# A one-core hybrid decoder trunk: the stores of activation pairs and their sums, in the up projection, go out on GpSimd's queue instead of SyncE's

## The chip, the cores and the metric

The kernel runs on one core of a Trainium2 chip. The metric is the device time of one execution, in microseconds (us). SyncE (SP) computes nothing here: it issues the kernel's DMA transfers, each after a wait for its semaphores, strictly in the order in which they stand on its queue. GpSimd (POOL), VectorE (DVE), ScalarE (ACT) and TensorE (PE) each run their own list of instructions, also in order.

## The reference, cut to what matters

One layer over 2048 tokens of width 1024: a mixer (sliding-window attention beside a gated recurrence), then a gated MLP of inner width 2816 with a causal convolution of three taps. Only the MLP matters here:

```python
h = rms_norm(x, ffn_norm_g[l]) * (1 + scale_f) + shift_f
u, v = jnp.split(h @ w_up[l], 2, axis=-1)          # 1024 -> 2 x 2816
u = causal_depthwise_conv(u, conv_w[l], conv_b[l])
x = x + gate_f * ((jax.nn.silu(u) * v) @ w_down[l])
```

## The kernel before, in words

All matmuls are made in float32 from a high and a low part of each operand: ScalarE rounds the high part (names ending in `h`), VectorE subtracts it for the low one (`l`), and three matmuls are added (`mm3`). Large products are split in 2 x 2 blocks and made with seven block products instead of eight, so that sums and differences of blocks have to be formed beforehand; GpSimd forms those of the weights.

**Up projection.** Two halves of 1024 tokens (`hf_`), and in each 22 blocks of 128 columns (`ff`) of both halves of w_up. For a column block, `prep_up` loads two raw weight tiles on SP (`wu_0r` and `wu_1r`, 512 KB each), GpSimd makes `s<-wu_1r`, `wu_1r<-wu_0r,wu_1r`, `s<-s,wu_0r` and, after VectorE has split them, a last `s<-wu_0r,s`. The splits are `wus`, `wvs`, `ws` and `w`. TensorE then runs seven products of 12 matmuls each into `ps_u`, in the order 1, 7, 2, 6, 5, 4, 3; product 1 uses `wus`, product 7 `wvs`. `up` adds the products, applies the convolution and the gate, and leaves the block's activations in `cc`.

**The pair of activations.** After every second block, `combine_a` forms on GpSimd the sums that the down projection's block products want: four operations, `sm<-cc,cc`, `cc<-cc`, `sm<-sm,cc`, `sm<-cc,sm`. Three stores follow, to a tensor in HBM, `act_d`, one for each pair: the second block `b` (512 KB), the first block `a`, which the second operation has changed (512 KB), and the three sums `sm` (768 KB). The first store needs nothing of GpSimd, the second its second operation, the third its fourth.

**What else is on these queues.** In half 1 `combine_w` makes the down projection's weight sums, one block for each `ff` up to 17 and two for each of 18 and 19: a load `cw` on SP, four operations `ct` on GpSimd, a store `wc_d` on SP. In half 0 `combine_t` does the like for the second half's inputs, four times. The raw tiles of `wu`, `cw` and `ct` share four buffers.

**Down projection.** It reads `act_d` (loads `da`) and the weights and their sums (loads `Sr` and `dw`, three to a block of weights), splits them (`S_0h`, `S_0l` and so on; `Th`, `Tl`) and multiplies into `ps_d`. Its first unit of work needs weights of all eleven blocks and the activations of half 0 only.

The order of instructions on each engine is made by a scheduler, which in the up projection is free to move what is independent; the numbers on a name (`act_d1_2`) are half and pair, on `cw0_7` output half and block.

Of the kernel before, what the change touches and what calls it, by code (L numbers as in the profile page):

```python
# [53 lines left out]
def kernel(ctx, tc, x, c, ada_w, ada_b, mix_norm_g, w_in, b_in, attn_sinks, attn_out_g,  # L54
# [3 lines left out]
    V, S, G, TE, SY = (InOrder(tc, e) for e in (nc.vector, nc.scalar, nc.gpsimd, nc.tensor, nc.sync))  # L58
# [21 lines left out]
    act_d = [[dram.tile([P, HT // 256, 7, P], F32, name=f"act_d{i}_{j}") for j in range(NJ)] for i in range(T // HT)]  # L80
# [1095 lines left out]
    def combine_acts(hf_, ff):  # L1176
        if len(acts) == 2:
            combine_a(hf_, ff // 2, *acts)
            acts.clear()

    def combine_a(hf_, j, c0, c1):


        a, b = (c.rearrange("p (t s n) -> p t s n", s=2, n=P) for c in (c0, c1))
        sm = gp_.tile([P, HT // 256, 3, P], F32, tag="gate", name=f"sm{hf_}_{j}")
        G.tensor_tensor(out=sm[:, :, 0, :], in0=a[:, :, 1, :], in1=b[:, :, 1, :], op=ALU.add)
        G.tensor_tensor(out=a[:, :, 1, :], in0=a[:, :, 0, :], in1=a[:, :, 1, :], op=ALU.subtract)
        G.tensor_tensor(out=sm[:, :, 1, :], in0=sm[:, :, 0, :], in1=a[:, :, 0, :], op=ALU.subtract)
        G.tensor_tensor(out=sm[:, :, 2, :], in0=b[:, :, 0, :], in1=sm[:, :, 1, :], op=ALU.subtract)
        for i, t in ((2, b), (0, a), (4, sm)):  # L1190
            SY.dma_start(out=act_d[hf_][j][:, :, i:i + (3 if i == 4 else 2), :], in_=t)

    def combine_t(k):

# [331 lines left out]
```

## Time and profile before

| | us |
|---|---|
| median of three runs | 2515.71 |
| lowest and highest of them | 2512.38, 2517.46 |
| the profiled execution's own time | 2515.02 |
| its span, from first to last instruction | 2513.2 |
| up projection, approximately | 1160 to 1992 of the span |
| down projection, approximately | 1997 to the end |

The mean granted clock of TensorE over the span was 0.970 of full speed. The profiled execution lies 0.69 us below the median and 1.8 us above its own span, so positions in the trace can be set directly against the times. Every store of `act_d` was issued by SP; GpSimd issued no transfer at all.

### The profile page before, as it was taken

To read this page: it belongs to the slowest core of one execution; us is meant where nothing else is said; L and a number is where in the kernel's file an instruction comes from. 1 tells how busy PE (TensorE), PEld (TensorE's weight loads), DVE (VectorE), ACT (ScalarE), POOL (GpSimd) and SP (SyncE) were. 2 spreads that over 40 slices of the span, in tenths; PEclk is the share of its full clock that TensorE was granted. 3 is DMA by queue.
4 is the path that set the end of the run, shared out by engine and by line. 5 is a ranking of instruction groups with operands and counts; after the bars stand their busy time and mean duration, and the time that the engine had idled before them with its cause. 6 is when DMAs were issued, how large, how long until landed. Compare 5 with 4: busy or idle time off the path is not lost.

```text
span 2513.2 us, 35666 instructions
## 1 busy us (share of the span) xinstructions
PE 2330.0 (93%) x13369; PEld 2013.4 (80%) x13369; DVE 1875.4 (75%) x2743; ACT 1057.2 (42%) x1776; POOL 880.9 (35%) x677
## 2 busy tenths in 40 slices
PE   5889898998989899999999998999999789998997
PEld 4778787887878788888888886778888579997997
DVE  8888778788876876578777778577776676677665
ACT  3336434623733454554333334233333254455443
POOL 6222212222312221215765653677777410011000
PEclk8999999999999999999999999999999889998999
DMA  7243233323322256654434436455545487787776
GB/s 211 89 118 97 80 90 95 94 67 101 97 65 82 86 179 222 230 190 125 138 122 142 122 109 201 138 156 159 159 147 159 136 306 231 214 279 261 261 245 201
DMA packets 361592, 389.90 MB, mean 155 GB/s; under 512 B 14069, under 2 KB 292555, under 8 KB 361419
## 3 DMA queue, kind: packets, MB, share of 16 engines
q1 hardware_dynamic: 361419, 387.62, 49.0%
q8 instruction: 105, 1.72, 0.3%
q14 instruction: 68, 0.56, 0.1%
HBM read 293.71 MB, written 93.86 MB: 154 GB/s over the span
## 4 chain that ended last, share of the span: by engine, by line
PE 60%; DVE 13%; DMA 10%; POOL 8%; issue 5%; ACT 3%; SPq 1%; DVEq 0%; ACTq 0%; POOLq 0%
PE ps_u L46 16%; PE ps_d L46 15%; PE ps_o L46 6%; PE lv L46 3%; PE ps_hg L46 3%; PE ps_hf L46 3%; PE ps_hq L46 3%; PE ps_i L46 2%; PE att_o L46 2%; POOL s L46 2%; DVE ada L46 2%; DMA Sr<-wc_d 1%; PE ps_q L46 1%; POOL wu_1r L46 1%; DVE AT L46 1%
## 5 line engine op out<-in xcount | busy, mean ns | idle before, releaser
L46 DVE TENSOR_TENSOR Tl<-da,Th 128x896 fp32r<-128x896 f32 x176 | 198.1, 1133 | 121.3 <-ACT Th L46 120.4
L46 ACT ACTIVATE Th<-da 128x896 fp32r<-128x896 f32 x176 | 166.3, 949 | 197.2 <-PE ps_d L46 158.8
L46 DVE SCALAR_TENSOR_TENSOR cc<-ub,cols,cc 128x1024 f32<-128x1024 f32 x88 | 150.1, 1706 | 19.6 <-ACT cc L46 17.4
L46 PE MATMUL lv<-a_q,K 128*128 128x128 f32 (+2 forms) x768 | 80.0, 264 | 44.4 <-DVE K L46 40.7
L46 PEld LDWEIGHTS lv<-a_q,K 128*128 128x128 f32 (+2 forms) x768 | 71.9, 176 | 56.9 <-DVE K L46 29.0
L46 POOL TENSOR_TENSOR s<-wu_0r,s 128x512 f32<-128x512 f32 x44 | 68.2, 1550 | 116.5 <-DVE ws_0l L46 14.8
L46 POOL TENSOR_TENSOR s<-wu_1r 128x512 f32<-128x512 f32 x44 | 69.7, 1584 | 87.8 <-DMA wu_1r<-in_w_up_dram 17.6
L46 ACT ACTIVATE cc<-cc 128x1024 f32<-128x1024 f32 x44 | 46.7, 1061 | 113.7 <-DVE cc L46 113.7
L46 DVE TENSOR_TENSOR cc<-cc,v 128x1024 f32<-128x1024 f32 x44 | 59.7, 1357 | 44.8 <-ACT cc L46 44.8
L46 POOL MEMSET AT<- 128x512 f32 x16 | 8.5, 533 | 232.1 <-PE ho L46 210.1
L46 POOL TENSOR_TENSOR wu_1r<-wu_0r,wu_1r 128x512 f32<-128x512 f32 x44 | 85.2, 1936 | 3.1
L46 POOL TENSOR_TENSOR pl<-raw,ph 128x512 fp32r<-128x512 f32 x32 | 45.4, 1419 | 101.2 <-ACT ph L46 85.6
L46 POOL TENSOR_SCALAR rv_d<-ssd 128x2 f32<-128x2 f32 x8 | 1.5, 193 | 209.3 <-DVE ssd L46 209.3
L46 POOL TENSOR_TENSOR s<-s,wu_0r 128x512 f32<-128x512 f32 x44 | 74.6, 1696 | 0.0
L46 DVE TENSOR_TENSOR v<-ps_u,v 128x512 f32<-128x512 f32 x88 | 60.4, 687 | 19.0 <-PE ps_u L46 15.7
L46 POOL TENSOR_TENSOR S_0l<-Sr,S_0h 128x512 fp32r<-128x512 f32 x1 | 2.6, 2600 | 202.2 <-ACT S_0h L46 202.2
L46 DVE COPY_PREDICATED AT<-lev,lv 128x512 f32<-128x512 uint32 (+1 forms) x96 | 69.8, 727 | 2.4 <-PE lv L46 1.2
L46 ACT ACTIVATE cc<-ub,cols 128x1024 f32<-128x1024 f32 x44 | 54.6, 1240 | 31.8 <-DVE ub L46 31.8
L46 DVE TENSOR_TENSOR ada<-ada,cond 128x1024 f32<-128x1024 f32 (+1 forms) x37 | 55.1, 1489 | 14.5 <-DMA ada<-in_ada_w_dram 13.1
L46 DVE TENSOR_TENSOR a_q<-a_q,tot 128x256 f32<-128x256 f32 x96 | 52.2, 544 | 11.8 <-PE lv L46 10.6
L46 DVE TENSOR_TENSOR ub<-ps_u,u 128x512 f32<-128x512 f32 x88 | 60.0, 682 | 0.1
L46 DVE TENSOR_TENSOR ot<-ps_o,gate 128x512 f32<-128x512 f32 x32 | 22.0, 688 | 47.7 <-PE ps_o L46 47.2
(2136 smaller groups left out, 9113.4 us busy)
## 6 DMA issues: line engine op xcount, KB each, us to landing
da<-act_d SPq DMA_DIRECT2D x176, 448.0 KB, 4.6
wu_0r<-in_w_up_dram SPq DMA_DIRECT2D x44, 512.0 KB, 3.7
wu_1r<-in_w_up_dram SPq DMA_DIRECT2D x44, 512.0 KB, 4.1
act_d<-cc SPq DMA_DIRECT2D x44, 512.0 KB, 5.9
ada<-in_ada_w_dram SPq DMA_DIRECT2D x40, 512.0 KB, 6.3
act_d<-sm SPq DMA_DIRECT2D x22, 768.0 KB, 4.7
x<-in_x_dram SPq DMA_DIRECT2D x26, 512.0 KB, 5.6
Sr<-wc_d SPq DMA_DIRECT2D x18, 512.0 KB, 7.1
```

Of the source, the lines that this page charges most:

```text
L46: ins = fn(*args, **kwargs)
```

## The change

One word: the three stores of `combine_a` are issued by `G` (GpSimd) instead of `SY` (SP). There are 66 of them, two `cc` and one `sm` for each of 22 pairs.

```diff
         for i, t in ((2, b), (0, a), (4, sm)):
-            SY.dma_start(out=act_d[hf_][j][:, :, i:i + (3 if i == 4 else 2), :], in_=t)
+            G.dma_start(out=act_d[hf_][j][:, :, i:i + (3 if i == 4 else 2), :], in_=t)
```

What the scheduler makes of it is seen in the order of instructions, here in three places. First SP's queue, in half 1, around the third pair (`act_d1_2`), before and after in one piece; the same piece recurs for every pair of half 1 up to the eighth.

```order
 L46 DMA wu1_8_0r_14678<-in_w_up_dram 128x8x128
 L46 DMA wu1_8_1r_14680<-in_w_up_dram 128x8x128
-L46 DMA act_d1_2_102<-cc1_5_14514 512x1x256
-L46 DMA act_d1_2_102<-cc1_4_14372 512x1x256
-L46 DMA act_d1_2_102<-sm1_2_14553 512x1x384
 L46 DMA cw0_7r_14812<-in_w_down_dram 128x2x512
 L46 DMA wc_d0_7_118<-ct0_7r_14814 128x1024
```

The load `cw0_7r`, which stood behind the three stores, now stands directly behind the weight load.

Second, GpSimd's list at the same pair.

```order
 L46 TENSOR_TENSOR s1_7_14536<-s1_7_14536,wu1_7_0r_14528 128x512
 L46 TENSOR_TENSOR sm1_2_14553<-cc1_4_14372,cc1_5_14514 128x4x128
+L46 DMA act_d1_2_102<-cc1_5_14514 512x1x256
 L46 TENSOR_TENSOR cc1_4_14372<-cc1_4_14372 128x4x128
 L46 TENSOR_TENSOR sm1_2_14553<-sm1_2_14553,cc1_4_14372 128x4x128
+L46 DMA act_d1_2_102<-cc1_4_14372 512x1x256
 L46 TENSOR_TENSOR sm1_2_14553<-cc1_5_14514,sm1_2_14553 128x4x128
+L46 DMA act_d1_2_102<-sm1_2_14553 512x1x384
 L46 TENSOR_TENSOR s1_7_14536<-wu1_7_0r_14528,s1_7_14536 128x512
 L46 TENSOR_TENSOR ct0_7r_14814<-cw0_7r_14812 128x256 x2
```

The three stores now stand among and behind the four sums, and ahead of the weight operations `s` and `ct` that come next. At the last pair of half 0 the operation `s1_1<-wu1_1_1r` stands ahead of the third store, elsewhere all three stand as here.

Third, SP's queue at the step from the up to the down projection.

```order
 L46 DMA da0_0_0_16944<-act_d0_0_89 128x896
-L46 DMA act_d1_10_110<-cc1_21_16833 512x1x256
-L46 DMA act_d1_10_110<-cc1_20_16724 512x1x256
-L46 DMA act_d1_10_110<-sm1_10_16839 512x1x384
 L46 DMA Sr0_1_16950<-in_w_down_dram 128x256
 L46 DMA Sr0_1_16950<-in_w_down_dram 128x512
```

The loads of the down projection's second block of weights (`Sr0_1`) and all behind them stood behind the stores of the last pair, and now stand behind none.

## Rows read from the trace of the kernel before

**Rows 1.** The page, part 1: busy us (share of the span) x instructions, one engine

```profile
PE 2330.0 (93%) x13369; PEld 2013.4 (80%) x13369; DVE 1875.4 (75%) x2743; ACT 1057.2 (42%) x1776; POOL 880.9 (35%) x677
```

**Rows 2.** Windows: us, busy of PE, PEld, DVE, ACT, POOL; clock, DMA share, GB/s

```profile
1380.00:1480.00 100.00, 100.00 (x439) 82.03 (x438) 78.69 (x84) 34.91 (x37) 61.91 (x37) 1.00 0.42 126
...
1680.00:1780.00 100.00, 99.35 (x434) 80.95 (x433) 74.57 (x78) 33.58 (x37) 79.29 (x53) 1.00 0.49 154
...
1980.00:2080.00 100.00, 75.00 (x471) 68.95 (x470) 68.58 (x64) 46.52 (x50) 16.64 (x10) 0.83 0.74 257
```

**Rows 3.** Waits of SP's queue, 1090 to 1985: total us, times, longest

```profile
SPq L46 <- DVE cc L46: 67.0, 8, 11.9
SPq L46 <- POOL cc L46: 62.7, 16, 5.4
...
SPq L46 <- POOL sm L46: 47.9, 25, 3.0
```

**Rows 4.** Timeline of SP's queue: start us, us, engine, line, operation, out<-in

```profile
1699.23 0.57 SPq L46 DMA_DIRECT2D cw_7r<-in_w_down_dram  x1
...
1988.03 0.36 SPq L46 DMA_DIRECT2D da<-act_d  x1
1996.65 4.94 SPq L46 DMA_DIRECT2D act_d<-cc  x2
2004.50 0.51 SPq L46 DMA_DIRECT2D act_d<-sm  x1
2005.07 1.67 SPq L46 DMA_DIRECT2D Sr<-in_w_down_dram  x2
```

**Rows 5.** Timeline of GpSimd; in brackets idle time before and what ended it

```profile
1567.90 2.02 POOL L46 TENSOR_TENSOR s<-wu_1r 128x512 f32<-128x512 f32 x1 [6.75 <-DMA wu_1r<-in_w_up_dram]
...
1616.43 2.28 POOL L46 TENSOR_TENSOR sm<-sm,cc 128x512 f32<-128x512 f32 x1
...
1627.14 1.43 POOL L46 TENSOR_TENSOR ct_3r<-cw_3r 128x256 f32<-128x256 f32 x2 [4.81 <-DMA cw_3r<-in_w_down_dram]
...
1695.05 1.30 POOL L46 TENSOR_TENSOR sm<-sm,cc 128x512 f32<-128x512 f32 x1
...
1704.64 1.92 POOL L46 TENSOR_TENSOR ct_7r<-cw_7r 128x256 f32<-128x256 f32 x2 [3.81 <-DMA cw_7r<-in_w_down_dram]
...
1709.02 1.29 POOL L46 TENSOR_TENSOR s<-wu_1r 128x512 f32<-128x512 f32 x1
...
1748.04 1.30 POOL L46 TENSOR_TENSOR s<-wu_1r 128x512 f32<-128x512 f32 x1
...
1943.89 2.51 POOL L46 TENSOR_TENSOR ct_9r<-cw_9r 128x256 f32<-128x256 f32 x2 [6.79 <-DMA cw_9r<-in_w_down_dram]
...
2003.20 1.28 POOL L46 TENSOR_TENSOR sm<-cc,sm 128x512 f32<-128x512 f32 x1
```

**Rows 6.** Timeline of TensorE in half 1

```profile
1572.40 0.80 PE L46 MATMUL ps_u<-t_T3h,wvs_1h 128*128 128x512 f32 x1 [7.53 <-ACT wvs_1h L46]
...
1675.07 0.51 PE L46 MATMUL ps_u<-t_T3h,wvs_6l 128*128 128x512 f32 x1 [0.32 <-DVE wvs_6l L46]
...
1909.18 0.50 PE L46 MATMUL ps_u<-t_T3h,wvs_18l 128*128 128x512 f32 x1 [0.30 <-DVE wvs_18l L46]
```

**Rows 7.** Timeline of ScalarE at the step to the down projection

```profile
2011.46 1.70 ACT L46 ACTIVATE S_1h<-Sr 128x1792 fp32r<-128x1792 f32 x1 [13.67 <-DMA Sr<-wc_d]
```

**Rows 8.** Timeline of VectorE at the same step

```profile
2013.19 2.02 DVE L46 TENSOR_TENSOR S_1l<-Sr,S_1h 128x1792 fp32r<-128x1792 f32 x1 [11.21 <-ACT S_1h L46]
```

**Rows 9.** One window of 10 us, columns as in Rows 2

```profile
2010.00:2020.00 10.00, 5.95 (x27) 5.81 (x28) 6.05 (x4) 6.38 (x5) 0.00 (x0) 0.51 1.03 400
```

**Rows 10.** Operations that touch act_d: duration ns min/median/max, first and last start

```profile
L46 SPq DMA_DIRECT2D act_d<-cc x44: 513/525/1247, 1163.2 to 2001.1; - x44
```

**Rows 11.** Timelines of VectorE and TensorE in half 0, at block 18

```profile
1453.05 1.22 DVE L46 TENSOR_TENSOR wvs_18l<-wu_1r,wvs_18h 128x1024 fp32r<-128x1024 f32 x1
...
1463.38 0.39 PE L46 MATMUL ps_u<-t_T3h,wvs_18l 128*128 128x512 f32 x1
```

## The prediction

> **What bounds the kernel now.** TensorE is busy 93% of the span [rows 1], but that share is an average, so I read the windows next. In half 0 it is busy 100 us of 100 at the full clock [rows 2]: nothing but fewer matmuls could shorten that stretch, and the change can only harm it. In half 1 it is busy 99.35 of 100, and GpSimd, at 79.29, is the fullest I see it. At the step to the down projection TensorE is busy 75 of 100, with the clock down to 0.83. So whatever can be gained lies in half 1 and at the two seams.
>
> Then the waits of SP's queue. Between 1090 and 1985 SP stood 67.0 us for `cc` of VectorE, 62.7 us for `cc` of GpSimd and 47.9 us for `sm` of GpSimd [rows 3]. Those are the operands of the moved stores. SP is otherwise idle enough, so the waits themselves cost nothing; they cost where a load that somebody wants stands behind them. The timelines show four kinds of such places:
>
> - *the step to the down projection.* SP issued the first block's loads by 1988.4, then stood for the last pair: stores at 1996.65 and 2004.50, the next weight load at 2005.07 [rows 4]. GpSimd's last sum began at 2003.20 and took 1.28 us [rows 5]: it is what released SP. ScalarE meanwhile stood 13.67 us for `Sr` [rows 7], VectorE 11.21 us for ScalarE's `S_1h` [rows 8].
> - *the seam of the halves.* GpSimd stood 6.75 us for `wu_1r`, which was issued behind the last pair of half 0; TensorE stood 7.53 us in the sequel [rows 5, 6].
> - *one early and one late pair of half 1*, where GpSimd stood 4.81 us for `cw_3r` and 6.79 us for `cw_9r` [rows 5].
> - *the steady pairs of half 1.* GpSimd stood 3.81 us for `cw_7r`, which SP issued at 1699.23, right behind the sums' store [rows 4, 5]. From one pair to the next the same operation on GpSimd comes at 1709.02 and 1748.04, so its loop takes 39.02 us; TensorE waits only 0.32 us once in a loop, for the low half that follows from GpSimd's work [rows 5, 6]; between the first of these waits and the last, both shown, lie five more, so there are seven such pairs. GpSimd thus sets the pace here, by a hair.
>
> **The change part by part.** It takes 66 issues off SP, some 0.53 us each [rows 10], 35 us in all; SP had idle time everywhere, so this by itself is worth nothing. It puts 66 issues on GpSimd, 3 for each pair. Call one issue's time on GpSimd *d*. No row shows d, since GpSimd issued nothing before. SP's shortest, 0.51 us [rows 10], is my lower bound. Of the rows on GpSimd itself, its sum over the same tile takes 1.30 us when it is undisturbed and 2.28 us when it is not, the same operation one pair apart [rows 5]. I take d = 1.3 us, because its undisturbed operation is the commonest row of GpSimd's own pace and lies between the ends, keep 2.28 us as the upper bound, and write 3d for a pair: 3.9 us at the value taken, 1.5 and 6.8 us at the ends.
>
> *(A) The step to the down projection.* `Sr0_1` no longer stands behind anything that waits. ScalarE's idle 13.67 us and VectorE's 11.21 us bound the gain [rows 7, 8]. Two things could take it back: VectorE, which ends its previous work 11.21 us before `S_1l` and is busy after it, and the transfers, which run at 400 GB/s there [rows 9], so that the last pair's 1.75 MB, now in the midst of them, cost some 4.4 us. The loads can start 16.7 us sooner (2005.07 less 1988.4); less 4.4 us that is 12.3. The two views agree, and I take −12 us, with 8 (the pair's transfers counted twice) and 13.7 (all of ScalarE's wait) as ends. Here d hardly counts: nobody waits for the last stores.
>
> *(B) The seam.* `wu_1r` is issued before the last pair is done, so the wait of 6.75 us goes, but GpSimd now spends 3d ahead of the operation that TensorE waits for: −(6.75 − 3.9) = −2.9 us.
>
> *(C) The two odd pairs.* In the same way −(4.81 − 3.9) = −0.9 and −(6.79 − 3.9) = −2.9 us.
>
> *(D) The seven steady pairs.* The load `cw` comes early, so 3.81 us go from GpSimd's loop and 3d are put in: 39.02 − 3.81 + 3.9 = 39.11, that is +0.1 us each, +0.6 us together. This is the term that d can turn. TensorE can win no more than its 0.32 us, so at d = 0.51 the seven give −2.2 us; at d = 2.28 each loses 6.84 − 3.81 = 3.0 us, +21 us together.
>
> *(E) Half 0.* Eleven pairs pay 3d too. GpSimd is busy 61.91 of 100 us there [rows 2], and its results are early: `wvs_18l` is written by 1454.27 and first read at 1463.38, 9.1 us later [rows 11]. 3.9 us hide under that, 6.8 us as well; the cover is gone at d = 3, and beyond that each pair would pay the excess.
>
> *(F) Buffers and the scheduler's small moves.* A store on GpSimd starts at its producer's end, not later than on SP; `cc` and `sm` come free no later. The few matmuls that changed places have the same operands. Zero, with nothing waiting on them.
>
> Sum: −12 − 2.9 − 0.9 − 2.9 + 0.6 = −18.1 us on the profiled 2515.02 us, that is 2496.9; the median of the runs is 0.69 us higher. I forecast 2497 us.
>
> At d = 0.51 the sum is −12 − 5.2 − 3.3 − 5.3 − 2.2 = −28, or 2487 us. At d = 2.28 it is −12 + 0.1 + 2.0 + 0.1 + 21.2 = +11, or 2526 us. All ten places together turn on 3d: without the TensorE floor the sum is −12 − 6.75 − 4.81 − 6.79 − 26.67 + 30d, which is nought at d = 1.90.
>
> The row of 2.28 us beside the row of 1.30 us [rows 5] shows that GpSimd is slowed when something else runs, and VectorE is busy 74.57 of 100 us there [rows 2]. The Trainium skill, "SBUF — State Buffer", section "SBUF: two separate sides", speaks against the change by name: GpSimd writes the descriptors of its own transfers, cannot while VectorE holds the port that they share, and a transfer of some 0.62 us was seen to take 3.1 us beside a VectorE copy. No run so far shows that for a transfer here. With 3.1 us for d the sum would be an estimate of −57 + 93 = +36 us, or 2551 us, by that page.
>
> **The rivals.**
>
> 1. *GpSimd becomes the bound of half 1 (slower).* The mechanism: GpSimd's issue is stretched as its operations are, d reaches 2.28, and the steady pairs, already paced by GpSimd, run 3 us longer each. For it: 79.29 busy of 100 and a loop that leaves TensorE 0.32 us short. Against it: of the six operations over a whole tile in [rows 5], four took 1.28 to 1.30 us and two 2.02 and 2.28. It decides from d = 1.9 on, and gives 2526 us.
> 2. *The seam to the down projection gives nothing.* The loads leave early, but the first unit is limited by VectorE and transfers in common, and what is won at `S_1h` is lost by the last block. For it: the DMA share is 1.03 in that stretch [rows 9]. Against: VectorE's idle time comes before its first work, not in its midst. It takes (A) out: −6.1 us, 2509 us. The Trainium skill, "DMA: Bandwidth & Descriptors", section "Issuing engines are not separate DMA queues", would have it so: a second issuer adds no bandwidth and saves only issue time. The trace shows a third thing, loads held behind a waiting store [rows 4], which that sentence does not weigh.
> 3. *GpSimd issues as cheaply as SP.* d = 0.51, 2487 us. For it: the same instruction. Against: nothing but that row.
>
> **How the numbers follow.** The forecast (d from 0.9 to 1.7, the step to the down projection won) 0.45; rival 1, 0.27; rival 2, 0.15; rival 3, 0.13. A measurement of this kernel tells 0.2%, about 5 us, from no change. Faster by more: the forecast, rival 3 and some 0.06 of rival 2, 0.64. Within: the rest of rival 2 and the mild end of rival 1 (d near 1.9), 0.12. Slower: 0.24. The range is 2486 to 2528 us, from the cheap end to the stretched one; some 0.05 lies below and 0.13 above. The likeliest case's own range is 2488 to 2510: d from 0.9 to 1.7 moves the sum by some 20 us.
>
> **What would show it.** SP's issue of `Sr0_1` right behind the first block's loads, and VectorE's wait for `S_1h` gone: (A) right; `S_1h` early but the first steady stretch of `ps_d` no earlier: rival 2. GpSimd's free time between `sm<-cc,sm` and the next `s`, divided by the stores there: d. The same `s<-wu_1r` from pair to pair at 38.7 to 39.2 us: (D) right; at 41 or more: rival 1. TensorE's wait for `wvs_1h` down from 7.53 to near 4.7: (B). Half 0 still at 100 of 100: (E). The prediction is wrong if d is above 1.9, or if a wait that no row shows (the new queue's own completions, a buffer that comes free late) stands on GpSimd, where all weight sums queue behind it.

## The result, and the profile after

The change made the kernel faster: 2493.07 us, median of four runs (2490.66 to 2494.71), against 2516.53 us of before in the same series (four runs, 2512.38 to 2517.46). The ratio is 0.9908, with a 95% interval of 0.9895 to 0.9922. The forecast was 2497 us. The profiled execution took 2490.66 us, its span 2488.9 us.

The total was met more nearly than its parts. Two terms were wrong in opposite directions: an issue costs GpSimd less than I took, and the step to the down projection gave 4.7 us of the 12 that I put down for it.

First the page after, part 1 and the two queues of part 3 (packets, megabytes, share of the 16 DMA engines).

```profile
PE 2323.8 (93%) x13369; PEld 2010.0 (81%) x13369; DVE 1911.0 (77%) x2743; ACT 1055.6 (42%) x1776; POOL 919.4 (37%) x743
...
q1 hardware_dynamic: 326571, 347.25, 44.8%
q0 software_dynamic: 10560, 40.37, 4.4%
```

The 66 stores now stand on GpSimd's list (743 instructions instead of 677) and on a queue of their own. VectorE, whose work is the same, is busy 35.6 us longer than in [rows 1].

The operations that touch `act_d`, after (duration in ns: least, median, most; first and last start):

```profile
L46 POOL DMA_DIRECT2D act_d<-cc x44: 692/724/893, 1160.2 to 1982.7; - x44
L46 POOL DMA_DIRECT2D act_d<-sm x22: 712/726/735, 1166.0 to 1986.1; - x22
```

This is *d*: 0.72 us, with little spread, against 0.51 to 0.53 us on SP [rows 10], and far from the 1.3 us taken.

Windows after, in three of the stretches of [rows 2], with the same columns:

```profile
1380.00:1480.00 100.00, 100.00 (x438) 82.02 (x437) 83.36 (x87) 35.13 (x37) 66.86 (x47) 1.00 0.43 135
...
1680.00:1780.00 100.00, 100.00 (x439) 81.98 (x438) 80.81 (x80) 32.77 (x36) 82.36 (x61) 1.00 0.50 162
...
1980.00:2080.00 100.00, 84.99 (x618) 81.51 (x618) 70.44 (x68) 46.86 (x55) 15.76 (x10) 0.89 0.79 265
```

Half 0 is full, as before. The steady stretch of half 1 has become full: TensorE 100.00 instead of 99.35. The third window, 1980 to 2080, has moved with the program and is no comparison in place.

To see where the time came from I set the first matmul of the same name side by side in both traces (starts in us, from TensorE's timelines):

| first matmul with | before | after | ahead by | gained since the line above |
|---|---|---|---|---|
| `wus_0h`, half 0: the up projection begins | 1111.30 | 1107.36 | 3.94 | (3.94) |
| `wvs_21h`, half 0 | 1520.59 | 1516.39 | 4.20 | 0.26 |
| `wvs_1h`, half 1: behind the seam | 1572.40 | 1561.48 | 10.92 | 6.72 |
| `wvs_5h`, half 1 | 1654.90 | 1642.18 | 12.72 | 1.80 |
| `wvs_19h`: behind the seven steady pairs | 1928.05 | 1911.35 | 16.70 | 3.98 |
| `S_0h` and `Th`: the down projection begins | 1997.84 | 1977.50 | 20.34 | 3.64 |
| `S_10h`, the last block of the first unit | 2051.74 | 2026.72 | 25.02 | 4.68 |
| end of the span | 2513.2 | 2488.9 | 24.3 | −0.7 |

The 3.94 us of the first line stand there before any store that was moved. They belong to one execution against another, not to the change: in the experiments below the same matmul began between 1110.5 and 1115.9. (The up projection begins there, near 1111; 1160, given in the table of times before, is about where its first store starts.) From there to `S_10h` the change gained 21.1 us, 20.4 to the end. The lines between hold within some 2 us: in `e9_after_again` below, the same kernel once more, the seam gave 4.4 us and the stretch to `wvs_5h` 3.2.

GpSimd's timeline after, at the pair of [rows 4, 5] that stores `act_d1_2` and at the late pair:

```profile
1676.38 2.30 POOL L46 TENSOR_TENSOR sm<-cc,cc 128x512 f32<-128x512 f32 x1
1678.63 0.72 POOL L46 DMA_DIRECT2D act_d<-cc  x1
...
1681.80 0.80 POOL L46 DMA_DIRECT2D act_d<-cc  x1
...
1684.47 0.73 POOL L46 DMA_DIRECT2D act_d<-sm  x1 [0.30 <-POOL sm L46]
...
1686.59 1.91 POOL L46 TENSOR_TENSOR ct_7r<-cw_7r 128x256 f32<-128x256 f32 x2
...
1691.95 1.29 POOL L46 TENSOR_TENSOR s<-wu_1r 128x512 f32<-128x512 f32 x1
...
1729.83 1.29 POOL L46 TENSOR_TENSOR s<-wu_1r 128x512 f32<-128x512 f32 x1
...
1920.25 2.71 POOL L46 TENSOR_TENSOR ct_9r<-cw_9r 128x256 f32<-128x256 f32 x2 [2.69 <-DMA cw_9r<-in_w_down_dram]
```

`ct_7r` no longer waits; the bracket of 3.81 us is gone. At the late pair 2.69 of 6.79 us are left. GpSimd's loop is 1729.83 − 1691.95 = 37.88 us, against 39.02. TensorE's own period, from `wvs_5h` to `wvs_19h` after, is (1911.35 − 1642.18) / 7 = 38.45 us. GpSimd is now the faster of the two.

At the seam TensorE's wait for `wvs_1h` fell from 7.53 to 2.85 us:

```profile
1561.48 0.79 PE L46 MATMUL ps_u<-t_T3h,wvs_1h 128*128 128x512 f32 x1 [2.85 <-ACT wvs_1h L46]
```

At the step to the down projection, first SP and then VectorE after:

```profile
1967.74 0.33 SPq L46 DMA_DIRECT2D da<-act_d  x1
1968.11 1.20 SPq L46 DMA_DIRECT2D Sr<-in_w_down_dram  x2
```

```profile
1981.52 3.10 DVE L46 TENSOR_TENSOR S_1l<-Sr,S_1h 128x1792 fp32r<-128x1792 f32 x1
1984.54 2.17 DVE L46 TENSOR_TENSOR Tl<-da,Th 128x896 fp32r<-128x896 f32 x1
1994.67 2.03 DVE L46 TENSOR_TENSOR S_2l<-Sr,S_2h 128x1792 fp32r<-128x1792 f32 x1 [7.96 <-issue]
```

The second block's loads are issued 0.04 us behind the first's, and VectorE's 11.21 us before `S_1l` [rows 8] are gone. But 7.96 us stand now one block further on, before `S_2l`, and the timeline names no producer for them ("issue"). That is where most of the missing gain went, and the experiments are built around it.

### The profile page after: what moved, and what is told of

Read it like the earlier page. It is cut to its first block, busy times and chain, and to the rows that moved or that the text cites. A ratio compares the mean times of both kernels' runs of the same rounds, so it can differ in the third digit from the quotient of the medians.

```text
span 2488.9 us, 35680 instructions
## 1 busy us (share of the span) xinstructions
PE 2323.8 (93%) x13369; PEld 2010.0 (81%) x13369; DVE 1911.0 (77%) x2743; ACT 1055.6 (42%) x1776; POOL 919.4 (37%) x743
## 3 DMA queue, kind: packets, MB, share of 16 engines
q1 hardware_dynamic: 326571, 347.25, 44.8%
q0 software_dynamic: 10560, 40.37, 4.4%
## 4 chain that ended last, share of the span: by engine, by line
PE 66%; DVE 13%; DMA 7%; POOL 6%; issue 5%; ACT 2%; SPq 0%; DVEq 0%; ACTq 0%; POOLq 0%
PE ps_u L46 24%; PE ps_d L46 15%; PE ps_o L46 5%; PE lv L46 3%; PE ps_hg L46 3%; PE ps_hq L46 2%; PE ps_hf L46 2%; PE ps_i L46 2%; PE att_o L46 2%; DVE ada L46 2%; DMA ada<-in_ada_w_dram 1%; POOL s L46 1%; PE ps_q L46 1%; DVE raw L46 1%; POOL sm L46 1%
## 5 line engine op out<-in xcount | busy, mean ns | idle before, releaser
L46 DVE TENSOR_TENSOR cc<-cc,v 128x1024 f32<-128x1024 f32 x44 | 64.9, 1476 | 44.5 <-ACT cc L46 44.5
L46 POOL TENSOR_TENSOR s<-wu_0r,s 128x512 f32<-128x512 f32 x44 | 59.3, 1347 | 107.4 <-DVE ws_0l L46 14.8
L46 POOL TENSOR_TENSOR wu_1r<-wu_0r,wu_1r 128x512 f32<-128x512 f32 x44 | 92.9, 2111 | 3.1
L46 DVE TENSOR_TENSOR v<-ps_u,v 128x512 f32<-128x512 f32 x88 | 60.4, 686 | 15.5 <-PE ps_u L46 12.2
```

Of the source, the lines that this page charges most:

```text
L46: ins = fn(*args, **kwargs)
```

## The experiments

Each kernel is compared with runs of before made beside it: 2514.96 us (median of 21) for e1 to e4, 2514.94 us (29) for e5 to e8, and 2515.62 us (7) for e9 to e11.

**One part of the change at a time.** Four kernels choose the queue by half and pair:

```diff
+            eng = G if CONDITION else SY
-            G.dma_start(out=act_d[hf_][j][:, :, i:i + (3 if i == 4 else 2), :], in_=t)
+            eng.dma_start(out=act_d[hf_][j][:, :, i:i + (3 if i == 4 else 2), :], in_=t)
```

`e6_half0_not_last`, condition `hf_ == 0 and j < NJ - 1`:

> Only the first ten pairs of half 0 store on GpSimd's queue: term (E) alone. The prediction says nought, since TensorE works back to back there: 2516 to 2517 us. The rival is the 4.2 us by which the changed kernel's trace is ahead already at block 18 of half 0: if that were the change's, this kernel would be 4 us faster, 2512; but 3.9 us of it stand there before the first moved store, so it should be one execution against another.

Measured: 2515.60 us, ratio 0.9998 (0.9989 to 1.0008). Half 0 gives nothing, as forecast, and the 4.2 us by which the trace after was ahead there were not the change's.

`e5_seam_only`, condition `(hf_, j) == (0, NJ - 1)`:

> Only the last pair of half 0 stores on GpSimd's queue: term (B) alone. By positions in the two traces 6.7 us, so 2510 us against 2516.5; the prediction's sum with the measured issue of 0.72 us gives 4.6 us, 2512.

Measured: 2507.77 us, ratio 0.9966 (0.9954 to 0.9978), 7.2 us faster; the interval, 5.5 to 11.6 us, leaves the prediction's 2.9 us out. The whole is near the 6.7 us of the table, but not the place: by positions against before, this kernel gains 3.6 us from `wvs_21h` to `wvs_1h` and 3.9 us more up to `wvs_5h`, where its own stores are as before.

`e4_half1_not_last`, condition `hf_ == 1 and j < NJ - 1`:

> Only the stores of the first ten pairs of half 1 begin on GpSimd's queue; half 0, the seam and the last pair stay as before. These are terms (C) and (D). Theory 1, by positions in the two traces: 1.8 us at the first pair, 4.0 us over the seven steady pairs, 3.6 us at the ninth, together 9 us, 2507 us. The prediction's sum with the measured issue of 0.72 us: 2.6, 2.2 and 4.6, likewise 9. If instead the gain of half 1 needs the earlier seam: under 5 us.

Measured: 2507.24 us, ratio 0.9967 (0.9955 to 0.9980), 7.7 us faster. Half 1 gains without the seam.

`e1_last_only`, condition `(hf_, j) == (1, NJ - 1)`:

> Only the three stores of the very last pair (half 1, pair 10) begin on GpSimd's queue; the other 63 stay on SP's. This is term (A) of the prediction alone. Theory 1, from the trace after: the loads of the down projection do leave some 16 us sooner, but VectorE's S_2l then stands 7.96 us until the last store has landed, because the tile that it writes lies on the memory of the last pair's sums; (A) is worth 4 to 5 us, so 2511 to 2513 us against 2516.5. Theory 2, the prediction's: 12 us, so 2504 to 2505.

Measured: 2510.54 us, ratio 0.9980 (0.9971 to 0.9988), 4.4 us faster, with 7.3 us as the far end of the interval. Theory 1 holds, the 12 us of the prediction don't. VectorE's timeline in this kernel shows the same wait as in the whole change:

```profile
2014.66 2.02 DVE L46 TENSOR_TENSOR S_2l<-Sr,S_2h 128x1792 fp32r<-128x1792 f32 x1 [7.69 <-issue]
```

The four parts add up to 7.2 + 7.7 + 4.4 − 0.7 = 18.6 us, close to the 20.4 us by which the trace after is ahead at its end once its first line is taken off.

**What `S_2l` waits for.** In the built program `S_2l` waits, beside its operands, for completions of stores to `act_d`, that of the last pair's `sm` among them. It writes memory that these stores read. The timeline names nobody for the wait, but two other views of the trace after do: who waited for operations on `act_d`, and what TensorE waited for (us, times; us, times, longest).

```profile
who waited for it (us, times):
...
  DVE S_2l L46: 8.0, 1
```

```profile
PE ps_d L46 <- DVE S_2l L46: 7.5, 1, 7.5
```

The last store had landed at 1994.39, and `S_2l` started at 1994.67; in e1 the two stand at 2014.49 and 2014.66. In the trace before, the last store had landed by 2008.96, and `S_2l` started only at 2016.98. Three kernels test whether that is the wait of 7.96 us.

`e2_place` gives the operand tiles other places. The list sets the order in which they are laid out:

```diff
-    S_PLACE = ("2h", "0h", "3h", "0l", "T", "1h", "1l", "2l", "3l", "4l", "5l", "6l", "7l", "6h", "7h", "4h", "5h")
+    S_PLACE = ("2h", "0h", "3h", "0l", "T", "1h", "1l", "6l", "7l", "2l", "3l", "5l", "4l", "6h", "7h", "4h", "5h")
```

> The changed kernel with the operand tiles of the down projection at other places in memory: the tiles of S_2l and S_3l change places with those of S_6l, S_7l, S_4l and S_5l, so that S_6l and S_7l, which are wanted some 15 us later, lie on the last pair's sums. The order of instructions on all engines is the same row for row. Theory 1 (S_2l waits for memory that the last store still reads): the wait of 7.96 us goes, S_2l starts near 1987 and 6 to 8 us are won, 2485 to 2487 us. Rival: the first unit is bound by VectorE and the transfers in any case, and the last block's S_10h comes no sooner; 2492 to 2494 us, as the changed kernel.

Measured: 2487.30 us, ratio to before 0.9892 (0.9876 to 0.9908), which overlaps the interval of the change itself. So it was run again beside the changed kernel (`e9_after_again`, `e10_place_again`):

> The changed kernel once more, beside e10 and e11 on the same chip, since e2_place had been set against it only over two series of runs. 2491 to 2495 us.

> e2_place once more. By positions in its trace the stretch from the first matmul of the down projection to S_10h is 42.85 us long, against 49.22 in the changed kernel, so it should be some 6 us below e9; if the gain of the places was one series against another, both come out within 2 us.

Measured: e9 2494.27 us (2493.93 to 2495.10, ratio to before 0.9915, 0.9900 to 0.9929), e10 2487.37 us (2486.83 to 2492.78, ratio 0.9891, 0.9875 to 0.9908). The places are worth 6.9 us by the medians; no e10 run was as slow as the fastest of e9. VectorE in e10:

```profile
1984.61 3.10 DVE L46 TENSOR_TENSOR S_1l<-Sr,S_1h 128x1792 fp32r<-128x1792 f32 x1
1987.63 2.17 DVE L46 TENSOR_TENSOR Tl<-da,Th 128x896 fp32r<-128x896 f32 x1
1989.72 2.01 DVE L46 TENSOR_TENSOR S_2l<-Sr,S_2h 128x1792 fp32r<-128x1792 f32 x1
...
1994.05 2.03 DVE L46 TENSOR_TENSOR S_3l<-Sr,S_3h 128x1792 fp32r<-128x1792 f32 x1 [1.31 <-issue]
```

`S_2l` starts behind `Tl` without a wait; 1.31 us are left before `S_3l`, which starts at 1994.05, when the last pair's second `cc` store has landed (1993.97). From the first matmul of the down projection to `S_10h` e10 takes 2022.63 − 1980.60 = 42.0 us, the changed kernel 49.2, before 53.9. The order of instructions was the same on every engine, so nothing but the addresses can have done it. The step is then worth 11.9 us: what the prediction gave it.

`e8_before_place` is the control, the same places in the kernel before:

> The kernel before, all stores on SP, with the places in memory of e2_place. The control for it: in the trace of before the last stores landed before S_2l was wanted, so the places should be worth nothing, 2515 to 2518 us. If it is faster by more than 3 us, the places help for another reason, and e2_place doesn't show what it was meant to.

Measured: 2514.78 us, ratio 0.9999 (0.9990 to 1.0008). The places alone are worth nothing; the wait for that memory was always in the program, but hidden behind the loads that SP held back.

`e11_place_less` is e10 with the condition `hf_ == 1 or j == NJ - 1`:

> e10, but the first ten pairs of half 0 store on SP's queue again, 30 issues fewer on GpSimd. Half 0 gave nothing by itself, so the time should be that of e10 within 2 us; if GpSimd's issues there cost VectorE time that TensorE feels, it is faster than e10, if SP's waits there matter, slower.

Measured: 2486.80 us, ratio to before 0.9883 (0.9867 to 0.9900). It equals e10, so half 0's stores are worth nothing here either, and it is the fastest median of the study, 7.5 us below e9.

**What an issue costs GpSimd.** `e3_twice` issues each store as two:

```diff
-            G.dma_start(out=act_d[hf_][j][:, :, i:i + (3 if i == 4 else 2), :], in_=t)
+            for q in (0, 2):
+                G.dma_start(out=act_d[hf_][j][:, q:q + 2, i:i + (3 if i == 4 else 2), :], in_=t[:, q:q + 2])
```

> The changed kernel with each store on GpSimd issued as two halves, so 6 issues for a pair instead of 3, with the same bytes. It tests what an issue costs GpSimd and at which point GpSimd becomes the bound of half 1. In the changed kernel three issues lengthened GpSimd's loop from 35.21 us (39.02 less the 3.81 us of waiting) to 37.86, that is 0.88 us for each, just under TensorE's 38.45. If the cost is by the issue: loop near 40.5, 2 us above TensorE's, 14 us for seven pairs, and some 4 to 6 us at the seam and the odd pairs, so 2510 to 2514 us. If the cost is by the rows moved: an issue takes 0.36 us, the loop stays at 37.9 and the time at 2493.

Measured: 2521.46 us, ratio 1.0023 (1.0014 to 1.0031): slower than before, and 27 to 28 us behind the change. Its issues and GpSimd's loop:

```profile
L46 POOL DMA_DIRECT2D act_d<-cc x88: 725/725/931, 1163.8 to 2014.8; - x88
L46 POOL DMA_DIRECT2D act_d<-sm x44: 725/725/727, 1170.7 to 2016.2; - x44
```

```profile
1702.95 1.45 POOL L46 DMA_DIRECT2D act_d<-sm  x2
...
1711.17 1.29 POOL L46 TENSOR_TENSOR s<-wu_1r 128x512 f32<-128x512 f32 x1
...
1750.84 1.29 POOL L46 TENSOR_TENSOR s<-wu_1r 128x512 f32<-128x512 f32 x1
```

An issue with half the bytes takes the same 0.725 us: the cost goes by the issue. The loop is 39.67 us, 1.22 above TensorE's 38.45, and seven pairs should lose 8.5 us; by positions against the trace after they lose 8.5 (14.43 us behind at `wvs_5h`, 22.95 at `wvs_19h`). That is rival 1, brought about with six issues instead of a dearer one. My figure missed on the seam: between `wvs_21h` of half 0 and `wvs_1h` this kernel loses 10.7 us, where three more issues make 2.2. The order of instructions on VectorE, ScalarE, SP and TensorE is that of the changed kernel; it is GpSimd that comes late. Set against the trace after, its first sum of a pair starts 3.6 us later at the first pair of half 0, 11.9 us later at the ninth, and 11.9 us later (1559.95) at the last, while TensorE stays 3.4 to 3.6 us behind up to `wvs_21h`. Half 0 thus hid six issues to a pair from TensorE, but VectorE's preparations for half 1 stand behind splits that wait for GpSimd's sums, and came late with them. That all of the 10.7 us comes from there was not tested.

**Another queue.** `e7_act_queue` has one word changed:

```diff
-            G.dma_start(out=act_d[hf_][j][:, :, i:i + (3 if i == 4 else 2), :], in_=t)
+            S.dma_start(out=act_d[hf_][j][:, :, i:i + (3 if i == 4 else 2), :], in_=t)
```

> All 66 stores on ScalarE's queue instead of SP's or GpSimd's. It tests whether leaving SP's queue is what pays, or where the stores go. ScalarE works only 42% of the time, but it isn't the producer: it must stand for GpSimd's sums before it goes on with the splits wvs_h and ws_h, and at the last pair before S_0h. If only leaving SP counts: 2492 to 2500 us. If the wait moves with the store: TensorE waits for wvs_h at every pair of half 1 and for Th and S_0h at the step to the down projection, and the time is at or above that of before, 2515 to 2540.

Measured: 2516.20 us, ratio 1.0000 (0.9992 to 1.0009). ScalarE's timeline in it, at a steady pair and at the step to the down projection:

```profile
1697.93 0.52 ACTq L46 DMA_DIRECT2D act_d<-cc  x1
1700.56 0.52 ACTq L46 DMA_DIRECT2D act_d<-sm  x1
1701.18 1.06 ACT L46 ACTIVATE ws_7h<-s 128x1024 fp32r<-128x1024 f32 x1 [7.07 <-DMA act_d<-cc]
...
2009.55 0.52 ACTq L46 DMA_DIRECT2D act_d<-sm  x1
2010.12 1.70 ACT L46 ACTIVATE S_0h<-Sr 128x1792 fp32r<-128x1792 f32 x1 [7.15 <-POOL sm L46]
```

An issue is 0.52 us here, cheaper than on GpSimd, yet nothing is won: before `ws_7h` ScalarE stands 7.07 us at the two stores that need GpSimd's sums, and `S_0h` stands behind the last of them. By positions `S_0h` comes 12.2 us later than before (the 2.6 us by which this execution began later taken off), and `S_10h` level with it. The wait went with the stores. On GpSimd it is next to nothing (the bracket of 0.30 us), since the stores stand behind the operations that make their data.

## Why the prediction was right, and where it was not

- **What holds the kernel back: right.** Loads stood on SP behind stores that waited. SP's 35 us of issue time were worth nothing where it can be seen by itself: e6 took 30 issues off SP and gained nothing. In e7, with all 66 off SP, ScalarE's new waits may hide a gain. The Trainium skill, "DMA: Bandwidth & Descriptors", "Issuing engines are not separate DMA queues", allows a second issuer only issue time; the runs show that what pays here is who waits: e7 and the change differ in one word, the issuing queue.
- **d: mis-sized, 0.72 us for 1.3.** In the loop three issues cost (37.88 − 35.21) / 3 = 0.89 us each, with the short wait of 0.30 us ahead of the third and longer operations beside it. The bound from SP's row was nearer than the row I chose; GpSimd's operations over a tile say nothing of its issues.
- **(B), 2.9 us: mis-sized.** At 0.72 us the sum would be 6.75 − 2.2 = 4.6. By positions up to `wvs_1h` 6.7 (after), 4.4 (e9) and 3.6 us (e5) were found; e5 as a whole gains 7.2, since the pair behind the seam gains too, which the prediction did not put down to the seam.
- **(C), 0.9 and 2.9 us: right way.** 1.8 and 3.6 by positions. At the second, the prediction let all of GpSimd's 6.79 us go, and 2.69 stayed. There TensorE's wait for `wvs_20h`, 4.3 us, went, and part of it came back at `ws_21l`, where the wait rose from 1.1 to 3.3 us.
- **(D), a loss of 0.6 us: wrong sign.** 4.0 us were gained, 0.57 for each pair. TensorE's period is 38.45 us, so it could win 0.57 us, not the 0.32 of the wait that I took from [rows 6]: the bracket counts only a part of what a loop of 39.02 us costs TensorE. How much of this falls to the seven pairs depends on the execution: in e1, e6 and e8, which have these pairs as before, TensorE runs the first two at 38.45 us and comes to 39.02 only behind them, 271.4 to 271.5 us for the seven against 273.2, and is 1.4 to 1.6 us longer over the pair ahead of them. The turning point stands: GpSimd has room for 38.45 − 35.21 = 3.2 us a pair, and e3 crossed it.
- **(E), nought: right** (e6).
- **(A), 12 us: right in mechanism, and undone by a step that I put at zero.** I wrote that "nobody waits for the last stores" and, in (F), that `cc` and `sm` come free no later, hence zero. They did come free sooner, 1994.39 against 2008.96, but the next writer of that memory now came sooner still: `S_2l` waits for the last store to have landed. GpSimd's last issue began at 1986.06 in the trace after and took 0.73 us; `S_2l` started at 1994.67. The step gave 4.7 us; with the tile elsewhere it gives 11.9. Rival 2 foresaw the symptom, not the cause: it was neither VectorE nor the transfers.
- **The total** came near by luck: (A) fell 7 us short while (B), (C) and (D) together brought 10 us more.
- **The rule against the change did not bear.** The Trainium skill, "SBUF — State Buffer", "SBUF: two separate sides", keeps GpSimd from writing descriptors while VectorE runs an operation in a 2-port mode, and says further on in that section that `tensor_tensor` has no such mode. The prediction took its 3.1 us, which was measured beside a copy, for a kernel whose issues lie beside `TENSOR_TENSOR` alone. With VectorE busy 80.81 of 100 us the longest of 66 issues took 0.89 us, though 43 of them ran wholly within one operation of VectorE. What the trace does show is VectorE's operations growing longer, told below.

## What to carry to other kernels

A store holds back whatever stands behind it on its queue, so it belongs on a queue whose own work it waits for: here the producer's, where the wait was 0.3 us, and not merely on a free one, where the same wait came back whole. Count issues, not bytes, when the producer is nearly the bound: here three to a pair cost the kernel nothing, and six made it slower than it had been. And when a transfer that everyone waited behind is taken out of the way, look at which memory it still reads and who will write there next: here the gain stopped at that tile until the tile was moved.

## What the runs showed of the hardware that was not expected

Nothing slowed GpSimd's issues, but VectorE's operations beside them grew longer. The same operation in half 0, before and then after:

```profile
1360.20 2.23 DVE L46 TENSOR_TENSOR ws_13l<-s,ws_13h 128x1024 fp32r<-128x1024 f32 x1
```

```profile
1356.00 4.09 DVE L46 TENSOR_TENSOR ws_13l<-s,ws_13h 128x1024 fp32r<-128x1024 f32 x1
```

GpSimd's timeline after, in the same moment:

```profile
1356.39 1.36 POOL L46 TENSOR_TENSOR cc<-cc 128x512 f32<-128x512 f32 x1
1357.65 1.35 POOL L46 TENSOR_TENSOR sm<-sm,cc 128x512 f32<-128x512 f32 x1
1358.87 0.81 POOL L46 DMA_DIRECT2D act_d<-cc  x1
```

Within VectorE's 4.09 us GpSimd ran two operations and an issue, each in about its usual time. Undisturbed neighbours of the same shape take 1.22 us. Over the run VectorE was busy 35.6 us more for 66 issues, and 15.0 us more for the 30 of e6 (1890.4 against 1875.4). But with the 132 of e3 it was 38.8 us more (1914.2), hardly above the 35.6: the growth does not go by the issue. Matched operation by operation, about half of it after (18.7 us) fell on operations that no issue touched. TensorE never felt it in half 0. That GpSimd's work holds VectorE's operations up is only inferred from the durations.

The queue also cut the stores differently. On SP's queue the 66 stores were (361419 − 326571) / 66 = 528 packets each; on GpSimd's they are 10560 / 66 = 160, and the median from issue to landing fell from 5.9 to 4.0 us for `cc` and from 4.7 to 4.2 for `sm`. No experiment separates this from the quieter moment at which they now start.
